# Decayed keys of a gated recurrence built by ACT in scaled blocks, and three GpSimd products moved to VectorE

## The chip, the cores and the metric

The kernel runs on one core of a Trainium2 chip. The metric is device time in microseconds (us) of one execution; the runs of the kernel before gave 2340.97, 2344.2 and 2345.61, with a median of 2344.2. The engines are named as in the profile: PE is TensorE's matmul, PEld its weight load, DVE VectorE, ACT ScalarE, POOL GpSimd, SP the engine that issues most DMAs.

## The reference

Two layers of a hybrid backbone work on 128 context tokens and 512 latent tokens of width 2048. Each layer normalises and modulates its input (adaLN), projects it to 6656 columns, and hands them to three groups of heads: windowed attention with rotary position (A), a gated linear recurrence in both directions (B), and a spatial gating MLP (C). Each branch is multiplied by its own gate and all are projected back. The change touches B and the rotary part of A. The recurrence, cut to what matters:

```python
def step(S, xs):                       # one chunk of 32 tokens
    qc, kc, vc, lfc = xs
    b = jnp.cumsum(lfc, axis=-2)
    qe = qc * jnp.exp(b)
    ke = kc * jnp.exp(-b)
    att = jnp.where(causal, jnp.einsum('bhtd,bhsd->bhts', qe, ke), 0.0)
    o = jnp.einsum('bhtd,bhdv->bhtv', qe, S) + jnp.einsum('bhts,bhsv->bhtv', att, vc)
    b_last = b[..., -1:, :]
    S = jnp.exp(b_last)[..., 0, :, None] * S + jnp.einsum('bhsd,bhsv->bhdv', kc * jnp.exp(b_last - b), vc)
    return S, o
```

and the rotary position of queries and keys of latent tokens:

```python
out = jnp.stack([x1 * cs - x2 * sn, x2 * cs + x1 * sn], axis=-2)
```

## The kernel before, in words

All 640 tokens (5 tiles of 128) stay on the chip. The input projection is split into blocks of columns. A block is either "rowmajor" (512 columns, tokens on the partitions of the result) or "colmajor" (128 columns, features on the partitions, tokens in halves of 384 and 256). Weights and inputs are each split in a high and a low part, and three matmuls make a product (L652 to L654, L660). The weight block `wr` comes by a DMA that SP issues, ACT rounds it to `wh` (L640), DVE subtracts to get `wl` (L641); four `wr` and three `wh` and `wl` buffers rotate.

All other work is laid beside this stream. A list `side` holds generators: the attention of a tile, the recurrence of a head, the gating MLP. The loops over weight blocks call `tick()`, which runs the first generator up to its next `yield`. A second list, the filler, makes the adaLN vectors of later use: DVE multiplies and adds blocks of `w_ada` as they land (L302, two of 512 columns for each block, 480 in all). The framework then orders each engine's instructions by priority (program order, with weight work raised) and by when it reckons the inputs ready; every engine runs its own list strictly in order. So a change of engine or of reckoned time moves instructions on all of them.

The recurrence handles a head at a time, four to a layer, with both directions d in one generator. `hgrn_prep` makes the cumulated gates, `qe` and the keys `e`, the chunk decays `Dt` (for each tile a 5x4 table a channel: how much chunk c's key has decayed for a query of chunk i), the end-of-tile decays `EG`, the keys `kd` for the state (L1044, DVE) and the queries `qB` for the state (L1045, POOL). Then the tile states are chained (L1067 transposes, L1068 copies on ACT, L1072 products, L1078 on DVE).

A loop over n makes the scores of tile n. A tile has four chunks of 32, and a query chunk i needs keys of chunks c <= i, decayed by `Dt[i, c]`. `build(j)` makes, for each direction, a buffer K of 128x512: four copies of the tile's 128 key columns, the i-th scaled chunk by chunk by row i of `Dt`; where c > i the factor is exp(-1e30), so 0, and where c = i it is 1. Before, this is one POOL product of 128x512 with broadcast operands (L1090). The score matmuls (L1105) take 32 query columns as weights and one of the four copies as moving data: four for each direction (two profile records each, as the operands are plain fp32). DVE keeps the causal part (L1108) and adds the directions (L1110); after one more yield PE transposes the sum (L1128), ACT copies it to `aT` (L1130), and three steps later the outputs are accumulated (L1117, L1120) and squared on ACT (L1123). There is one K buffer for each direction, so `build(n + 1)`, called right after the score matmuls of n, waits until they have read it. At the end the head's outputs are scaled on DVE (L1137), transposed on PE (L1143) and multiplied into the gate buffer B.

Three more products stand on POOL before: the two halves of rope (L751; DVE makes their terms in L748 and L749), the gate of each head in `b_gate` (L1004: B times the sigmoid), and `qB`. The sigmoid itself (`sigma`) is a minimum on DVE (L227), then a logarithm and an exponential on ACT (L228, L229). Elsewhere POOL multiplies the gates of the other branches (L1211), splits some activations (L622, L1229), scales the MLP (L1178, L1179) and adds the output (L1260).

## Time and profile before

| | |
|---|---|
| median of the runs | 2344.2 us |
| the profiled execution | 2338.18 us |
| its span, first to last instruction | 2336.4 us |
| PE busy | 2261.4 us (97%) |
| PEld busy | 1968.0 us (84%) |
| DVE busy | 1424.3 us (61%) |
| ACT busy | 778.7 us (33%) |
| POOL busy | 293.9 us (13%) |
| mean granted PE clock | 0.988 |

The span leaves out 1.8 us around the first and last instruction. PE's busy time is that of pipelined matmuls, whose records overlap: a stretch can show PE busy throughout and still run at different rates. A group's row gives its busy time in us, the mean of one in ns, then how long its engine had been idle before it and what ended that. In a row of the timeline the first number is the start, the second the duration from the first start to the last end of the merged instructions.

### The profile page before, as it was taken

How to read it: one execution, taken by the hardware profiler on the slowest of the kernel's cores; microseconds unless marked ns; L12 is line 12 of the kernel's file. 1: busy time of each engine (PE TensorE's matmuls, PEld its weight loads, DVE VectorE, ACT ScalarE, POOL GpSimd, SP SyncE). 2: the span in 40 equal slices, each digit the busy share in tenths (PEclk: the TensorE clock that was granted, in tenths of full speed). 3: DMA queues.
4: the chain of work that ended last, by engine and by line, in shares of the span. 5: the costliest groups of instructions: out<-in, count | busy, mean ns of one | idle time of the engine just before them, and what ended most of it. 6: DMA issues, size and time to landing. Idle time of an engine off the chain costs nothing.

```text
span 2336.4 us, 34944 instructions
## 1 busy us (share of the span) xinstructions
PE 2261.4 (97%) x13308; PEld 1968.0 (84%) x13308; DVE 1424.3 (61%) x2612; ACT 778.7 (33%) x1605; POOL 293.9 (13%) x234
## 2 busy tenths in 40 slices
PE   7999999999999989989999999999999999999999
PEld 5766678899999888977787878799999998998887
DVE  3436987768887766666667455855875942434223
ACT  3323434343334322332224234344343332223111
POOL 0000111002122211011112010101222220101110
PEclk9999999999999999999999999999999999999999
DMA  9675632434433354355552221322332323324332
GB/s 321 218 254 191 209 117 83 148 95 120 126 117 104 111 163 144 111 192 171 173 170 91 77 68 47 115 68 72 111 94 76 114 90 92 103 75 149 106 106 84
DMA packets 264876, 296.41 MB, mean 127 GB/s; under 512 B 17378, under 2 KB 166772, under 8 KB 262916
## 3 DMA queue, kind: packets, MB, share of 16 engines
q1 hardware_dynamic: 254368, 271.27, 37.2%
q10 hardware_dynamic: 10340, 22.91, 3.2%
q8 instruction: 104, 1.70, 0.3%
q14 instruction: 64, 0.52, 0.1%
HBM read 280.38 MB, written 13.73 MB: 126 GB/s over the span
## 4 chain that ended last, share of the span: by engine, by line
PE 75%; DVE 12%; DMA 7%; issue 2%; ACT 1%; POOL 0%; DVEq 0%; ACTq 0%; POOLq 0%
PE m L660 29%; PE m L652 11%; PE m L653 11%; PE m L654 11%; DMA wa<-in_w_ada_dram 6%; DVE aacc L302 4%; DVE wl L641 2%; PE s L240 2%; PE s L895 1%; PE s L941 1%; PE s L1105 1%; PE s L1072 1%; PE s L953 1%; PE s L954 1%; PE s L319 1%
## 5 line engine op out<-in xcount | busy, mean ns | idle before, releaser
L641 DVE TENSOR_TENSOR wl<-wr,wh 128x512 fp32r<-128x512 f32 (+1 forms) x535 | 401.5, 752 | 575.2 <-ACT wh L640 566.7
L640 ACT ACTIVATE wh<-wr 128x512 fp32r<-128x512 f32 (+1 forms) x535 | 336.1, 629 | 971.0 <-PE m L654 557.2
L652 PE MATMUL m<-wh,hh 128*128 128x512 f32 x1440 | 571.6, 397 | 9.2 <-DVE mg L1208 5.3
L653 PE MATMUL m<-wl,hh 128*128 128x512 f32 x1440 | 568.5, 395 | 3.5 <-DVE wl L641 3.5
L654 PE MATMUL m<-wh,hl 128*128 128x512 f32 x1440 | 565.6, 393 | 0.0
L660 PE MATMUL m<-hh,wh 128*128 128x384 f32 x2016 | 478.1, 317 | 0.0
L660 PE MATMUL m<-hl,wh 128*128 128x384 f32 x2016 | 465.0, 311 | 0.0
L660 PE MATMUL m<-hh,wl 128*128 128x384 f32 x2016 | 464.6, 311 | 0.0
L302 DVE SCALAR_TENSOR_TENSOR aacc<-wa,s,aacc 128x512 f32<-128x512 f32 x480 | 368.6, 801 | 72.9 <-DMA wa<-in_w_ada_dram 72.3
L652 PEld LDWEIGHTS m<-wh,hh 128*128 128x128 f32 x1440 | 272.0, 189 | 84.5 <-issue 10.3
L653 PEld LDWEIGHTS m<-wl,hh 128*128 128x128 f32 x1440 | 272.7, 189 | 64.2 <-DVE wl L641 7.4
L654 PEld LDWEIGHTS m<-wh,hl 128*128 128x128 f32 x1440 | 272.4, 189 | 59.0 <-issue 2.6
L660 PEld LDWEIGHTS m<-hh,wh 128*128 128x128 f32 x2016 | 312.5, 190 | 9.8 <-issue 8.1
L660 PEld LDWEIGHTS m<-hl,wh 128*128 128x128 f32 x2016 | 311.5, 189 | 0.4
L660 PEld LDWEIGHTS m<-hh,wl 128*128 128x128 f32 x2016 | 311.1, 189 | 0.3
L1090 POOL TENSOR_TENSOR mg<-ev,Dt 128x512 f32<-128x512 f32 x80 | 95.7, 1213 | 321.5 <-PE s L1105 107.2
L1260 POOL TENSOR_TENSOR mg<-mg,ev 128x512 f32<-128x512 f32 x30 | 43.9, 1473 | 287.9 <-DVE ev L1258 287.1
L751 POOL TENSOR_TENSOR mg<-g,g 128x256 f32<-128x256 f32 x32 | 32.8, 1047 | 263.8 <-DVE g L749 145.5
L925 ACT ACTIVATE g<-g,st,qs 128x384 f32<-128x384 f32 (+1 forms) x64 | 48.1, 752 | 36.0 <-DVE st L921 36.0
L228 ACT ACTIVATE ev<-ev 128x640 f32<-128x640 f32 x40 | 29.5, 738 | 72.3 <-DVE ev L227 71.2
L945 DVE TENSOR_TENSOR g<-s,g 128x512 fp32r<-128x512 f32 x56 | 38.4, 687 | 24.0 <-ACT g L944 18.1
L1045 POOL TENSOR_TENSOR g<-g,EG 128x512 f32<-128x512 f32 x16 | 22.7, 1416 | 239.4 <-DVE Dt L1030 125.1
(272 smaller groups left out, 1984.6 us busy)
## 6 DMA issues: line engine op xcount, KB each, us to landing
wr<-in_w_in_dram SPq DMA_DIRECT2D x406, 256.0 KB, 2.9
wa<-in_w_ada_dram SPq DMA_DIRECT2D x278, 256.0 KB, 3.0
wr<-in_w_out_dram SPq DMA_DIRECT2D x128, 256.0 KB, 2.9
wa<-in_w_ada_dram SPq DMA_DIRECT2D x16, 1024.0 KB, 6.7
wa<-in_w_in_dram SPq DMA_DIRECT2D x9, 1024.0 KB, 6.5
wa<-in_w_ada_dram SPq DMA_DIRECT2D x44, 128.0 KB, 3.3
mg<-const_xT_dram SPq DMA_DIRECT2D x4, 1280.0 KB, 5.8
x<-mg SPq DMA_DIRECT2D x20, 256.0 KB, 2.1
```

The source lines that it names most:

```text
L240: return self.nc.tensor.matmul(acc[32 * q:32 * q + 32, 0:n], lhsT=lhs[:, kk, :], rhs=rhs, start=kk < 4, stop=kk >= 12, skip_group_check=True)
L302: nc.vector.scalar_tensor_tensor(acc[:, cd], r, sc, acc[:, cd], op0=ALU.mult, op1=ALU.add)
L640: nc.scalar.activation(wh, raw, AF.Copy)
L641: nc.vector.tensor_tensor(wl, raw, wh.bitcast(F32), op=ALU.subtract)
L652: nc.tensor.matmul(ps, lhsT=hh, rhs=wh[:, 0], start=k == 0, stop=False)
L653: nc.tensor.matmul(ps, lhsT=hh, rhs=wl[:, 0], start=False, stop=False)
L654: nc.tensor.matmul(ps, lhsT=hl, rhs=wh[:, 0], start=False, stop=k == KT - 1)
L660: self.nc.tensor.matmul(ps[hf][:, 0:n], lhsT=w[:, a], rhs=h[:, o:o + n], start=k == 0 and i == 0, stop=k == KT - 1 and i == 2)
L925: nc.scalar.activation(dst[h], src[h], AF.Exp, bias=nmx[:, h:h + 1], scale=rq[:, h:h + 1], accum_out=den[:, h:h + 1])
L945: nc.vector.tensor_tensor(pt[1], pb, pt[0].bitcast(F32), op=ALU.subtract)
L1090: nc.gpsimd.tensor_tensor(k.rearrange("p (i c s) -> p i c s", i=4, c=4), bc(c4(pre[d][0])[:, j], 1, 4), bc(dd, 3, 32), op=ALU.mult)
L1260: (nc.vector if c == 3 else nc.gpsimd).tensor_tensor(xs, xs, y, op=ALU.add)
```

## The change

`build` no longer uses POOL. K's upper blocks (c > i) are zeroed once a layer by a DVE memset over both K buffers, since nothing writes there any more. For each key buffer ACT makes one copy of the four diagonal blocks (the key chunks unscaled, L1090 after) and six copies of 128x32 with a per-channel factor, one for each block below the diagonal (L1094). That is 14 ACT instructions a step in place of two POOL products; with 40 steps, 560 for 80. The rope halves, the gate and `qB` keep their form and move from POOL to DVE. Lines behind L1090 move down by three: L1105 is L1108 after, L1128 is L1131, L1143 is L1146.

```diff
@@ rope_ap
         for b, op in ((0, ALU.subtract), (1, ALU.add)):
-            nc.gpsimd.tensor_tensor(w(out)[:, :, :, b], w(t1)[:, :, :, b], w(t2)[:, :, :, b], op=op)
+            nc.vector.tensor_tensor(w(out)[:, :, :, b], w(t1)[:, :, :, b], w(t2)[:, :, :, b], op=op)
@@ b_gate
-        nc.gpsimd.tensor_tensor(self.B[:, h], self.B[:, h], s, op=ALU.mult)
+        nc.vector.tensor_tensor(self.B[:, h], self.B[:, h], s, op=ALU.mult)
@@ hgrn_prep
-        nc.gpsimd.tensor_tensor(c4(qB)[:, 1:5], c4(qe)[:, 1:5], bc(eg, 3, 32), op=ALU.mult)
+        nc.vector.tensor_tensor(c4(qB)[:, 1:5], c4(qe)[:, 1:5], bc(eg, 3, 32), op=ALU.mult)
@@ hgrn
             self.Cm = self.mg().rearrange("p (h t) -> p h t", h=4)
+            nc.vector.memset(self.Cm[:, 0:2, 0:512], 0.0)
@@ build
                 k = self.Cm[:, d, 0:512]
-                dd = pre[d][3][:, j, 0:4]
-                if d:
-                    dd = dd[:, :, ::-1]
-                nc.gpsimd.tensor_tensor(k.rearrange("p (i c s) -> p i c s", i=4, c=4),
-                                        bc(c4(pre[d][0])[:, j], 1, 4), bc(dd, 3, 32), op=ALU.mult)
+                blk = k.rearrange("p (a s) -> p a s", s=32)
+                e, dd = c4(pre[d][0])[:, j], pre[d][3][:, j]
+                nc.scalar.activation(blk[:, 3:13:3] if d else blk[:, 0:16:5], e[:, ::-1] if d else e, AF.Copy)
+                for i in range(1, 4):
+                    for c in range(i):
+                        q = 3 - c if d else c
+                        nc.scalar.activation(blk[:, 4 * i + q], e[:, q], AF.Copy, scale=dd[:, i, c:c + 1])
```

The order of the instructions, at the second score step of the second head in layer 0. First PE before: `mg` is K, `g` is `qe` of the one and the other direction, and `m` with `wh` and `wl` the weight stream.

```order
L660 MATMUL m_6033<-hh_1022,wl_6158 128x384
L660 MATMUL m_6034<-hh_1022,wl_6158 128x256
L1105 MATMUL s_6195<-mg_4873,g_5741 32x128 x4
L1105 MATMUL s_6201<-mg_4873,g_5949 32x128 x4
L660 MATMUL m_6033<-hh_1032,wh_6157 128x384
L660 MATMUL m_6034<-hh_1032,wh_6157 128x256
L660 MATMUL m_6033<-hl_1033,wh_6157 128x384
L660 MATMUL m_6034<-hl_1033,wh_6157 128x256
L660 MATMUL m_6033<-hh_1032,wl_6158 128x384
L660 MATMUL m_6034<-hh_1032,wl_6158 128x256
L319 MATMUL s_6217<-ones,aacc_5372 128x1 x8
```

And the same place on PE now:

```order
L660 MATMUL m_6094<-hh_1022,wl_6231 128x384
L660 MATMUL m_6095<-hh_1022,wl_6231 128x256
L1108 MATMUL s_6280<-mg_4873,g_5802 32x128 x4
L660 MATMUL m_6094<-hh_1032,wh_6230 128x384
L660 MATMUL m_6095<-hh_1032,wh_6230 128x256
L660 MATMUL m_6094<-hl_1033,wh_6230 128x384
L660 MATMUL m_6095<-hl_1033,wh_6230 128x256
L660 MATMUL m_6094<-hh_1032,wl_6231 128x384
L660 MATMUL m_6095<-hh_1032,wl_6231 128x256
L1108 MATMUL s_6286<-mg_4873,g_6010 32x128 x4
L319 MATMUL s_6314<-ones,aacc_5409 128x1 x8
```

The score matmuls of the two directions stood together; now six matmuls of the weight stream stand between them. Of the 40 steps, 28 are parted so, by 1 to 14 matmuls; before, none was.

ACT from the same step on, before (`aT` is the transposed score, `junk` the square of an output):

```order
L640 ACTIVATE wh_6296<-wr_6294 128x512
L640 ACTIVATE wh_6355<-wr_6353 128x512
L987 ACTIVATE ev_6228<-m_6033 128x384
L987 ACTIVATE ev_6228<-m_6034 128x256
L1130 ACTIVATE aT_6253<-s_6251 128x128
L228 ACTIVATE ev_6228<-ev_6228 128x640
L229 ACTIVATE ev_6228<-ev_6228 128x640
L640 ACTIVATE wh_6414<-wr_6412 128x512
L1130 ACTIVATE aT_6308<-s_6306 128x128
```

and now, from the third step's first key on:

```order
L640 ACTIVATE wh_6476<-wr_6474 128x512
L987 ACTIVATE ev_6325<-m_6094 128x384
L987 ACTIVATE ev_6325<-m_6095 128x256
L1090 ACTIVATE mg_4873<-ev_5025 128x4x32
L1094 ACTIVATE mg_4873<-ev_5025,Dt_5812 128x32 x6
L1090 ACTIVATE mg_4873<-ev_5211 128x4x32
L1094 ACTIVATE mg_4873<-ev_5211,Dt_6020 128x32 x6
L228 ACTIVATE ev_6325<-ev_6325 128x640
L640 ACTIVATE wh_6535<-wr_6533 128x512
L229 ACTIVATE ev_6325<-ev_6325 128x640
L1133 ACTIVATE aT_6350<-s_6348 128x128
L1090 ACTIVATE mg_4873<-ev_5025 128x4x32
```

The 14 key instructions of a step now stand in ACT's list between the weight casts, the evacuation of the next head's gate (L987) and its sigmoid (L228, L229), so a key of the next step waits behind whatever these wait for.

## The prediction

> **What bounds the kernel now.** I read the head of the page first, then the waits of PE, then the busy time by stretches, then the groups that the change touches, and last the timeline of one recurrence step.
>
> ```profile
> span 2336.4 us, 34944 instructions
> PE 2261.4 (97%) x13308; PEld 1968.0 (84%) x13308; DVE 1424.3 (61%) x2612; ACT 778.7 (33%) x1605; POOL 293.9 (13%) x234
> ```
>
> PE is busy for 97% of the span, so an edit that adds no matmul can gain only from PE's idle time (75 us in all) and from the slow clock that follows a stall. The next view is who PE waited for (total us, times, longest).
>
> ```profile
> PE s L1143 <- DVE g L1137: 10.4, 6, 6.1
> ...
> PE s L941 <- DVE g L930: 8.7, 6, 3.2
> PE s L1072 <- ACT g L1068: 7.7, 2, 4.1
> ...
> PE s L1128 <- DVE att L1108: 1.9, 1, 1.9
> ...
> PE s L833 <- POOL g L751: 0.3, 1, 0.3
> ```
>
> Two things stand here. PE hardly ever waits for POOL: 0.3 us. POOL's key building (L1090), which the change takes away, ends no wait of PE at all. And where PE waits in the recurrence and the attention, the engine named is mostly DVE. So the moved work is not on the path; it can matter only by what POOL does to DVE, and by what ACT and DVE do with the work that they take over.
>
> ```profile
> 404.00:408.00 4.00, 0.89 (x7) 0.62 (x5) 2.11 (x8) 2.86 (x11) 0.30 (x1) 1.00 0.24 91
> 408.00:410.00 2.00, 1.92 (x8) 1.84 (x9) 0.61 (x4) 0.39 (x1) 0.00 (x0) 0.52 0.38 112
> 410.00:412.00 2.00, 2.00 (x6) 0.93 (x4) 0.69 (x1) 0.73 (x2) 0.00 (x0) 0.62 0.16 59
> ```
>
> These are stretches around one 3.2 us stall (PE, PEld, DVE, ACT, POOL busy, then the granted clock). After it the clock is 0.52 and 0.62 for two stretches of 2 us: 0.96 + 0.76 = 1.7 us more are lost. A stall of a few us therefore costs about half as much again.
>
> **What leaves POOL.**
>
> ```profile
> L1090 POOL TENSOR_TENSOR mg<-ev,Dt 128x512 f32<-128x512 f32 x80 | 95.7, 1213 | 321.5 <-PE s L1105 107.2 <-DVE ev L1039 94.7 <-issue 83.9
> ...
> L751 POOL TENSOR_TENSOR mg<-g,g 128x256 f32<-128x256 f32 x32 | 32.8, 1047 | 263.8 <-DVE g L749 145.5 <-PE s L955 92.8 <-issue 25.5
> ...
> L1045 POOL TENSOR_TENSOR g<-g,EG 128x512 f32<-128x512 f32 x16 | 22.7, 1416 | 239.4 <-DVE Dt L1030 125.1 <-issue 114.3
> ...
> L1004 POOL TENSOR_TENSOR mg<-mg,ev 128x640 f32<-128x640 f32 x8 | 13.7, 1711 | 60.4 <-ACT ev L229 38.9 <-DVE g L1037 13.6 <-DVE aacc L302 7.9
> ...
> L751 POOL TENSOR_TENSOR g<-g 128x128 f32<-128x128 f32 x16 | 9.3, 592 | 303.3 <-DVE g L749 257.8 <-issue 40.6 <-PE m L654 4.3
> ```
>
> 95.7 + 32.8 + 22.7 + 13.7 + 9.3 = 174 us of POOL's 294, or 59%.
>
> **What that gives back to DVE.** For the DVE lines that run beside POOL, the mean of a group stands above its median or its minimum; I read the excess as time held up by POOL.
>
> ```profile
> L641 DVE TENSOR_TENSOR wl<-wr,wh 128x512 fp32r<-128x512 f32 (+1 forms) x535 | 401.5, 752 | 575.2 <-ACT wh L640 566.7
> ...
> L302 DVE SCALAR_TENSOR_TENSOR aacc<-wa,s,aacc 128x512 f32<-128x512 f32 x480 | 368.6, 801 | 72.9 <-DMA wa<-in_w_ada_dram 72.3
> ```
> ```profile
> L1110 DVE TENSOR_TENSOR asum<-att,att 128x128 f32<-128x128 f32 x40 | 24.1, 603 | 0.8
> ...
> L1044 DVE TENSOR_TENSOR g<-ev,Dt 128x640 f32<-128x640 f32 x16 | 18.3, 1142 | 0.8 <-ACT Dt L1032 0.7
> ...
> L748 DVE TENSOR_TENSOR g<-mg,rope 128x256 f32<-128x256 f32 x32 | 17.6, 550 | 0.0
> ...
> L748 DVE TENSOR_TENSOR g<-ev,rope 128x128 f32<-128x128 f32 x16 | 4.9, 307 | 0.1
> ```
>
> The same lines with minimum/median/maximum (ns):
>
> ```profile
> L641 DVE TENSOR_TENSOR wl<-wr,wh x535: 415/692/2057, 34.0 to 2322.2; 128x512 fp32r<-128x512 f32 x178, 128x256 fp32r<-128x256 f32 x1
> ```
> ```profile
> L302 DVE SCALAR_TENSOR_TENSOR aacc<-wa,s,aacc x480: 715/745/2064, 207.3 to 1861.5; 128x512 f32<-128x512 f32 x160
> ```
> ```profile
> L1110 DVE TENSOR_TENSOR asum<-att,att x40: 264/739/1137, 571.5 to 1886.6; 128x128 f32<-128x128 f32 x40
> ```
> ```profile
> L1044 DVE TENSOR_TENSOR g<-ev,Dt x16: 811/826/1675, 533.1 to 1857.8; 128x640 f32<-128x640 f32 x16
> ```
> ```profile
> L748 DVE TENSOR_TENSOR g<-mg,rope x32: 408/417/960, 288.8 to 1479.4; 128x256 f32<-128x256 f32 x32
> ```
>
> 535 x (752 - 692) = 32; 480 x (801 - 745) = 27; 40 x (603 - 264) = 14; 16 x (1142 - 826) = 5; 32 x (550 - 417) = 4, and as much for L749, its twin: 86 us. Shared out by POOL's busy time, the moved operations own 59% of it: 51 us. The new DVE work is 32 rope halves at 0.417 = 13 us, 16 of the keys' rope at 0.307 = 5, 16 products of 512 columns at 0.826 x 512/640 = 0.66, so 11, 8 gates of 640 columns at 0.826 = 7, and two memsets that I bound by 1 us each: 38 us. DVE comes out about 13 us lighter, all of it in the recurrence; in the rope stretches it is even, since four operations at 0.55 become six at 0.417 (2.2 against 2.5 us a tile).
>
> The Trainium skill, "SBUF — State Buffer", section "Who interferes with whom", says that a VectorE operation with two SBUF inputs and a GpSimd operation that reads SBUF exclude each other wholly, the second waiting until the first has finished. The trace agrees only in part: L1110 goes from 264 to a median of 739 ns, a hold-up of 0.48 us, which is less than half of a POOL operation of 1.2 us. By the rule the relief could be as much as the 174 us of POOL time; by the rows it is 51.
>
> **What of it reaches PE.** The 1.9 us at L1128 is a late DVE (L1108) just beside key builds: I take -1.9 (0 to -1.9). Of the 10.4 us at L1143, 6.1 are one wait, and there DVE was in adaLN adds (L302), which wait for their own DMA (72.3 us); of the other 4.3 I take -3 (0 to -10.4 for the whole). The 7.7 us at L1072 come through ACT's L1068, queued behind a gate that waits for DVE, again behind L302: 0 (0 to -7.7). The 8.7 at L941 follow the rope bursts, which do not get shorter: 0 (-8.7 to +3, the latter if the burst, 0.3 us a tile longer in 8 of its tiles, lands on PE). Sum -4.9, with half as much again for the clock: **-7.3 us**.
>
> **What the split keys cost PE.** By the new order, PE runs the four score matmuls of direction 0, then other matmuls, then those of direction 1, in 28 of the 40 steps; before they stood together in all 40. The load rows show what a change of kind costs:
>
> ```profile
> 650.05 0.30 PEld L660 LDWEIGHTS m<-hh,wl 128*128 128x128 f32 x2
> 650.55 0.39 PEld L1105 LDWEIGHTS s<-mg,g 128*32 128x32 f32 x16 [0.20 <-issue]
> 651.14 0.30 PEld L660 LDWEIGHTS m<-hh,wh 128*128 128x128 f32 x2 [0.20 <-issue]
> ```
>
> Entering and leaving the group idles the loads 0.20 us each. A split adds one entry and one exit; as matmuls overlap loads, I take one of the two: 28 x 0.20 = **+5.6 us** (0, if the array hides both, to 28 x 0.40 = 11).
>
> **What ACT takes.** 80 copies of four blocks and 480 scaled blocks of 128x32, a shape that the trace of before doesn't have.
>
> ```profile
> L640 ACT ACTIVATE wh<-wr 128x512 fp32r<-128x512 f32 x533 | 335.3, 630 | 971.0 <-PE m L654 557.2 <-PE m L660 326.2 <-issue 30.5
> ...
> L382 ACT ACTIVATE hh<-mg,gs 128x512 fp32r<-128x512 f32 x16 | 11.3, 708 | 0.0
> ...
> L382 ACT ACTIVATE hh<-mg,gs 128x128 fp32r<-128x128 f32 x16 | 6.3, 391 | 9.0 <-DVE gs L288 9.0
> ...
> L1033 ACT ACTIVATE EG<-G 128x25 f32<-128x25 f32 x16 | 3.5, 220 | 4.5 <-DVE G L1027 4.5
> ```
>
> L382 scales by a column, as the new blocks do. Its two forms give (708 - 391)/384 = 0.83 ns a column, so 32 columns take 391 - 96 x 0.83 = 0.31 us; L1033, without a scale column, bounds it from below at 0.22, L382 from above at 0.39. Four unscaled blocks: 391 less 78 (708 - 630, the price of the column) = 0.31 too. Neighbours overlap:
>
> ```profile
> 662.28 0.28 ACT L1123 ACTIVATE junk<-s 128x128 bf16<-128x128 f32 x1 [2.48 <-PE s L1117]
> 662.46 0.19 ACT L1123 ACTIVATION_READ_ACCUMULATOR junk<-s 128x1 f32 x1
> ```
>
> The second starts 0.18 after a first of 0.28, so 0.10 is hidden, and a block occupies ACT 0.21 us. The Trainium skill, "ScalarE: Activation LUTs", section "What ACT_TABLE_LOAD costs", gives 186 ns + 0.833 ns a column, 93 more for a pointer operand and 93 of overlap; by that estimate it is 0.21 as well, and the sum would not change. No run here shows the new shape yet.
>
> A step has two keys: 14 x 0.21 = 2.9 us. Beside them ACT does a weight cast (0.63 - 0.10), aT (0.18) and the square with its accumulator (0.27): 3.9 us. PE's step:
>
> ```profile
> 648.02 0.38 PEld L1105 LDWEIGHTS s<-mg,g 128*32 128x32 f32 x16 [0.20 <-issue]
> ```
> ```profile
> 656.77 0.65 PE L1105 MATMUL s<-mg,g 128*32 128x128 f32 x16
> ```
> ```profile
> 661.18 0.64 PE L1105 MATMUL s<-mg,g 128*32 128x128 f32 x16
> ```
>
> 4.41 us from group to group, but only 650.55 - 648.02 = 2.5 from the first to the second. In the long steps ACT fits with 0.5 us over; in the short one direction 1's key is about 0.3 + 2.9 = 3.2 us after the first group and so late by 0.7, which the new order covers by 3 to 9 other matmuls (0.15 each, from 0.30 a pair). I take **0** for PE's waits on keys, because the row nearest to the new form is L382 and its step fits; the cover is 0.5 us a step, and the upper end is rival 2's. ACT grows by 560 x 0.21 = 118 us, a third on its 779.
>
> **The sum.** -7.3 + 5.6 + 0 = -1.7 us on the profiled execution (2338.18, of which 2336.4 are the span). The median of the runs is 2344.2, 6.0 above that execution; the difference is carried over: 2344.2 - 1.7 = 2342.5, so **2342 us**. About 0.2%, 4.7 us, is what a measurement of this kernel can tell from no change. The ends of the terms give (1.9 + 4.3 + half of 8.7) x 1.5 = -15.8 with free splits at best, and +11 with no relief at worst; as both ends seldom come whole, the forecast's own range is 2331 to 2353.
>
> **Rival 1, faster: the port frees DVE's whole queue.** If POOL holds DVE up more than my excess shows, the backlog behind which L1137, L1068 and L1108 stand goes too. The condition is that the adaLN adds come earlier, and with them their buffers and their next DMAs. Price: (10.4 + 7.7 + 1.9) x 1.5 = 30, less 5.6 for the splits: -24, so 2320 us. For it: L302 has a maximum of 2064 ns against a median of 745. Against it: 72.3 us of waits that are DMA's. By the skill's exclusive lock, named above, this would be the case; the trace bears it out in half, so 0.2.
>
> **Rival 2, slower: ACT's queue makes the keys late.** ACT runs in order, and gates of the next head stand between the builds.
>
> ```profile
> ACT ev L228 <- DVE ev L227: 71.2, 35, 5.5
> ```
>
> A gate waits 2.0 us for DVE on average, and now keys are queued behind it, for which PE waits; POOL had no such neighbour. It decides where ACT's step passes 4.41 us: with blocks at 0.25 instead of 0.21 the 0.5 us are gone, and without any overlap 14 x 0.31 + 0.63 + 0.28 + 0.47 = 5.7 us make 1.3 us x 24 long steps + about 1 x 8 short ones = 39 us. Half of that, or a 2 us gate in 10 of the 40 steps, is +20: 2364 us. Chance 0.2.
>
> **Rival 3: nothing comes back.** DVE's lateness is the DMA's alone and stays where it is; the splits cost 5.6: 2350 us, on the edge between no change and slower. Chance 0.1.
>
> **How the numbers follow.** Forecast 0.5, rivals 0.2, 0.2, 0.1. The forecast's range lies by 0.2 below 2339.5, by 0.25 within and by 0.05 above 2348.9; rival 3 gives half to each side of that edge. Faster: 0.2 + 0.2 = 0.40; same: 0.25 + 0.05 = 0.30; slower: 0.05 + 0.2 + 0.05 = 0.30. The range reaches to the middles of rivals 1 and 2, with a tenth beyond either: 2320 to 2364.
>
> **What would show it.** Right: L1110 near 264 ns throughout, L641 and L302 near their medians; L1094 at about 0.31 us and 0.21 apart; PE's wait at L1131 (now L1128) gone, no wait of PE on an ACT key above 1 us; L1108 in groups of eight. Wrong: PE waiting for L1094 in most steps, with the clock falling after it (rival 2), or the waits at L1146 and L1075 (now L1143 and L1072) gone as well (rival 1). A stall of a new kind in the attention would be outside all four.

## The result, and the profile after

The changed kernel takes 2316.97 us (median of 4 runs, 2315.74 to 2319.98) where the kernel before took 2342.59 (4 runs, 2340.47 to 2345.61): a ratio of 0.9892, with a 95% interval of 0.9874 to 0.9909. That is 25.6 us faster, where 2342 had been forecast with a range down to 2320. The profiled execution took 2315.77 us. The head of its page:

```profile
span 2313.9 us, 35246 instructions
...
PE 2255.9 (97%) x13308; PEld 1958.9 (85%) x13308; DVE 1391.7 (60%) x2686; ACT 894.0 (39%) x2165; POOL 120.6 (5%) x82
```

DVE took over 74 instructions and is busy for 32.6 us less. ACT grew by 115 us (118 was forecast), and PE's time is not longer for it. The waits of PE (total us, times, longest):

```profile
PE m L652 <- DVE mg L1211: 6.2, 1, 6.2
PE s L1146 <- DVE g L1140: 6.0, 2, 5.4
PE s L1196 <- DVE mg L1197: 5.4, 1, 5.4
PE s L1073 <- ACT g L1069: 4.1, 2, 2.2
...
PE s L941 <- DVE g L930: 1.3, 4, 0.4
```

L1146 is L1143 of before: 10.4 us have become 6.0. L1073 was L1072: 7.7 have become 4.1. The 8.7 us at L941 have become 1.3. The first and third rows stood at 5.3 and 5.1 us before (behind L1208 and L1194 there). The rows of the operations that the change touches, and of those beside them:

```profile
L302 DVE SCALAR_TENSOR_TENSOR aacc<-wa,s,aacc 128x512 f32<-128x512 f32 x480 | 354.6, 770 | 76.9 <-DMA wa<-in_w_ada_dram 76.2 <-DVE wl L641 0.5
...
L1094 ACT ACTIVATE mg<-ev,Dt 128x32 f32<-128x32 f32 x480 | 113.0, 309 | 9.4 <-PE s L1108 9.2
...
L748 DVE TENSOR_TENSOR g<-mg,rope 128x256 f32<-128x256 f32 x32 | 13.4, 418 | 0.0
L751 DVE TENSOR_TENSOR mg<-g,g 128x256 f32<-128x256 f32 x32 | 12.2, 419 | 0.1
...
L1113 DVE TENSOR_TENSOR asum<-att,att 128x128 f32<-128x128 f32 x40 | 11.5, 288 | 0.6
```

ACT's new blocks alone, with minimum, median and maximum (ns), and who waited for them (us, times):

```profile
L1094 ACT ACTIVATE mg<-ev,Dt x480: 302/307/323, 529.1 to 1863.1; 128x32 f32<-128x32 f32 x160
...
  PEld s L1108: 5.3, 27
```

L748 runs at 418 ns in the mean (550 before), the sum of the scores (L1113, L1110 before) at 288 (603 before), and the new blocks at 309 ns, the forecast 0.31 us. DMA's own share of L302's waits is what it was (76.2 us against 72.3).

**Where the time went.** Set beside each other at the same weight matmul, the two executions run level up to 280 us. The changed one is 10 us ahead by 530 us (first attention), 17 ahead by 1340 (recurrence), 20 by 1400 (second attention), 22.4 by 1895, and then keeps its lead. Two things make that up. The gaps in which neither PE nor PEld runs, added up from the instruction records, fell from 60.4 to 43.6 us: 16.8. And PE was at half clock in 16 windows of 3.41 us before, in 11 now: 5 windows, each worth half its length, 8.5 us. Together 25.3; the span lost 22.5, which leaves 2.8 us by which PE's work itself got longer.

### The profile page after: what moved, and what is told of

Read it like the earlier page. It is cut to its first block, busy times and chain, and to the rows that moved or that the text cites. A ratio compares the mean times of both kernels' runs of the same rounds, so it can differ in the third digit from the quotient of the medians.

```text
span 2313.9 us, 35246 instructions
## 1 busy us (share of the span) xinstructions
PE 2255.9 (97%) x13308; PEld 1958.9 (85%) x13308; DVE 1391.7 (60%) x2686; ACT 894.0 (39%) x2165; POOL 120.6 (5%) x82
## 4 chain that ended last, share of the span: by engine, by line
PE 53%; DVE 6%; DMA 3%; issue 1%; ACT 1%; DVEq 0%; ACTq 0%
PE m L660 21%; PE m L653 9%; PE m L652 9%; PE m L654 9%; DMA wa<-in_w_ada_dram 3%; DVE aacc L302 2%; DVE wl L641 1%; PE s L895 1%; PE s L941 1%; PE s L1108 1%; DVE ev L1261 0%; PE s L319 0%; PE s L1196 0%; PE s L953 0%; PE s L954 0%
## 5 line engine op out<-in xcount | busy, mean ns | idle before, releaser
L641 DVE TENSOR_TENSOR wl<-wr,wh 128x512 fp32r<-128x512 f32 (+1 forms) x535 | 386.9, 725 | 569.2 <-ACT wh L640 562.3
L302 DVE SCALAR_TENSOR_TENSOR aacc<-wa,s,aacc 128x512 f32<-128x512 f32 x480 | 354.6, 770 | 76.9 <-DMA wa<-in_w_ada_dram 76.2
L660 PEld LDWEIGHTS m<-hh,wh 128*128 128x128 f32 x2016 | 311.1, 189 | 13.6 <-issue 12.1
L1094 ACT ACTIVATE mg<-ev,Dt 128x32 f32<-128x32 f32 x480 | 113.0, 309 | 9.4 <-PE s L1108 9.2
L1214 POOL TENSOR_TENSOR mg<-mg,ev 128x640 f32<-128x640 f32 x16 | 26.6, 1663 | 1513.8 <-ACT ev L229 1493.2
L944 ACT ACTIVATE g<-s 128x512 fp32r<-128x512 f32 x56 | 32.5, 596 | 57.5 <-PE s L941 54.1
L945 DVE TENSOR_TENSOR g<-s,g 128x512 fp32r<-128x512 f32 x56 | 38.4, 688 | 23.4 <-ACT g L944 17.0
L1111 DVE COPY_PREDICATED att<-m,s 128x128 f32<-128x128 uint8 x80 | 22.8, 301 | 39.8 <-PE s L1108 39.0
```

The lines of the kernel that those rows point to most:

```text
L302: nc.vector.scalar_tensor_tensor(acc[:, cd], r, sc, acc[:, cd], op0=ALU.mult, op1=ALU.add)
L641: nc.vector.tensor_tensor(wl, raw, wh.bitcast(F32), op=ALU.subtract)
L660: self.nc.tensor.matmul(ps[hf][:, 0:n], lhsT=w[:, a], rhs=h[:, o:o + n], start=k == 0 and i == 0, stop=k == KT - 1 and i == 2)
L944: nc.scalar.activation(pt[0], pb, AF.Copy)
L945: nc.vector.tensor_tensor(pt[1], pb, pt[0].bitcast(F32), op=ALU.subtract)
L1094: nc.scalar.activation(blk[:, 4 * i + q], e[:, q], AF.Copy, scale=dd[:, i, c:c + 1])
```

## The experiments

Theory 1: POOL's two-input products hold up DVE's, and DVE's late results stop PE; taking the products off POOL gives that time back, whoever does them. Theory 2: the gain comes from the new order of instructions and shorter chains, and the hold-up is off the path. Each ratio is to the kernel before on the same chip.

| run | what | median us | before us | ratio, 95% interval |
|---|---|---|---|---|
| p_rope | before, rope to DVE | 2321.45 | 2341.93 | 0.9912 (0.9900 to 0.9925) |
| p_gates | before, gates and queries to DVE | 2337.0 | 2341.93 | 0.9975 (0.9963 to 0.9986) |
| p_keys | before, keys to ACT | 2340.53 | 2341.93 | 0.9988 (0.9979 to 0.9997) |
| hog | after, scratch products of the operands on POOL | 2342.33 | 2341.93 | 0.9996 (0.9987 to 1.0005) |
| hog_results | after, scratch products of the results on POOL | 2332.89 | 2338.73 | 0.9970 (0.9960 to 0.9980) |
| hog_writes | after, memsets on POOL, too many | 2373.02 | 2338.73 | 1.0135 (1.0117 to 1.0153) |
| hog_writes2 | after, memsets on POOL | 2312.82 | 2341.7 | 0.9881 (0.9864 to 0.9897) |
| hog_rope | after, scratch products beside rope alone | 2338.94 | 2341.7 | 0.9985 (0.9971 to 1.0000) |
| rope_w1 | before, rope's products on POOL made short writes | 2329.05 | 2340.66 | 0.9954 (0.9940 to 0.9967) |
| rope_w3 | the same, long writes | 2328.64 | 2340.66 | 0.9947 (0.9935 to 0.9959) |
| k3 | after, one more key buffer | 2309.14 | 2338.73 | 0.9868 (0.9850 to 0.9887) |
| keys_dve | after, keys on DVE | 2309.54 | 2341.7 | 0.9865 (0.9850 to 0.9881) |
| allv_keysdve | keys_dve, POOL empty | 2290.96 | 2341.7 | 0.9786 (0.9770 to 0.9802) |
| allv_k3 | k3, POOL empty | 2287.47 | 2338.73 | 0.9778 (0.9760 to 0.9795) |

### One part of the change alone

p_rope:

```diff
-            nc.gpsimd.tensor_tensor(w(out)[:, :, :, b], w(t1)[:, :, :, b], w(t2)[:, :, :, b], op=op)
+            nc.vector.tensor_tensor(w(out)[:, :, :, b], w(t1)[:, :, :, b], w(t2)[:, :, :, b], op=op)
```

> The kernel before, with one part of the change alone: the 32 half products of rope (L751) go from GpSimd to VectorE; gates, queries and keys stay on GpSimd. The two traces show that the time was gained in two kinds of stretch: about 13 us in the two attentions (280-530 us and the like in layer 1), about 9 us net in the recurrences. Theory 1 (hold-up: GpSimd's two-input products hold up VectorE's and are themselves held up, the worst of them 3746 ns, and the late result reaches TensorE through ScalarE): rope alone brings the attention's 13 us, so 2327 to 2333 us against 2342.6. Theory 2 (the prediction's term: the rope bursts only change hands, VectorE's own work takes the place of what it waited): 2340 to 2345 us. The order on TensorE changes a little here too (808 of 12,405 instructions stand elsewhere), so a gain does not yet tell hold-up from order; another run of this set does.

p_gates:

```diff
-        nc.gpsimd.tensor_tensor(self.B[:, h], self.B[:, h], s, op=ALU.mult)
+        nc.vector.tensor_tensor(self.B[:, h], self.B[:, h], s, op=ALU.mult)
...
-        nc.gpsimd.tensor_tensor(c4(qB)[:, 1:5], c4(qe)[:, 1:5], bc(eg, 3, 32), op=ALU.mult)
+        nc.vector.tensor_tensor(c4(qB)[:, 1:5], c4(qe)[:, 1:5], bc(eg, 3, 32), op=ALU.mult)
```

> The kernel before, with one part of the change alone: the gate products (L1004) and the decayed queries (L1045) go to VectorE. The order on TensorE is that of before, instruction for instruction, so any difference is of when things get ready. Theory 1 (hold-up): these 24 instructions carried some 22 of the 108 us by which VectorE's instructions beside GpSimd ran over their own free median, and the waits of TensorE on VectorE in the recurrence (L1146 behind L1140 10.4 us, L1072 behind L1069 7.7) shrink in part: 2 to 5 us are gained, 2337.5 to 2340.5 us. Theory 2 (hold-up off the path): within 1.5 us of 2342.6.

p_keys is the change's memset and its `build`, and nothing else:

```diff
-                nc.gpsimd.tensor_tensor(k.rearrange("p (i c s) -> p i c s", i=4, c=4),
-                                        bc(c4(pre[d][0])[:, j], 1, 4), bc(dd, 3, 32), op=ALU.mult)
+                nc.scalar.activation(blk[:, 3:13:3] if d else blk[:, 0:16:5], e[:, ::-1] if d else e, AF.Copy)
...
+                        nc.scalar.activation(blk[:, 4 * i + q], e[:, q], AF.Copy, scale=dd[:, i, c:c + 1])
```

> The kernel before, with one part of the change alone: the decayed keys as scaled block copies on ScalarE; rope, gates and queries stay on GpSimd. The key products of TensorE come apart in the same way as in the full change (28 of 40 steps in two groups of four). Theory 1 (hold-up): the 40 products of L1090 were the largest holder of VectorE in the recurrence (28 of 108 us); with them gone L1110 is back near 290 ns and the recurrence gains 6 to 10 us less 5.6 us for the groups that come apart: 2336 to 2343 us. Theory 2 (the recurrence loses only the 5.6 us of the split groups, nothing comes back): 2347 to 2349 us. A queue on ScalarE that makes keys late would show as TensorE waiting for L1094 in many steps and 2355 us or more.

Measured: rope alone gains 0.88%, 20.5 us, more than even theory 1 gave it. The gates and queries gain 0.25%, the keys 0.12%. The three add up to 1.25%, where the whole change gives 1.08%. Rope, 42 us of the 174 us that left POOL, brings four fifths of the gain; the keys, 96 us of it, gain next to nothing once the split groups are paid for (5.9 us, below). p_gates has PE's order of before, instruction for instruction, so its 0.25% owes nothing to PE's order. The remaining long waits of PE in p_rope are those of the recurrence:

```profile
PE s L1143 <- DVE g L1137: 11.3, 7, 6.8
PE s L166 <- DVE g L159: 9.7, 1, 9.7
PE s L1072 <- ACT g L1068: 7.0, 2, 3.7
```

L941 and L252 are gone from its first waits: in neither attention is there a gap of PE above 0.4 us, where before has 1.7 us at 296, 0.7 at 329, 3.2 at 405, 1.5 at 452 and 3.2 at 1383.

### Putting POOL's reads back, in the order of after

hog leaves the changed kernel as it is and makes POOL read the same operands into a tile that nobody uses:

```diff
             nc.vector.tensor_tensor(w(out)[:, :, :, b], w(t1)[:, :, :, b], w(t2)[:, :, :, b], op=op)
+            for i in range(nh // 2):
+                nc.gpsimd.tensor_tensor(self.hog.rearrange("p (h a e) -> p h a e", h=2, a=2),
+                                        w(t1)[:, 2 * i:2 * i + 2, :, b], w(t2)[:, 2 * i:2 * i + 2, :, b], op=op)
...
+                for i in range(4):
+                    nc.gpsimd.tensor_tensor(self.hog.rearrange("p (c s) -> p c s", c=4), e, bc(dd[:, i, 0:4], 2, 32), op=ALU.mult)
```

> The full change, and beside each product that it moved GpSimd reads the same operands again and writes products of them into a scratch tile that nobody uses (4 products of 128x128 for each key block, 5 for each gate, 4 for each decayed query, 1 or 2 for each half of rope). Order on TensorE and VectorE is that of the full change, instruction for instruction; GpSimd's reads are put back, its results are no longer waited for. Theory 1, in full (hold-up of VectorE by GpSimd's reads is what was gained): VectorE's instructions beside the scratch products run at 0.5 to 1.2 us again and most of the time comes back: 2330 to 2342 us against 2317.0 of the full change. Theory 1b (what was gained is the late results of GpSimd itself, the chain through them): VectorE runs long again but the time stays near 2317 to 2322. Theory 2 (the new order on TensorE brought the gain): 2315 to 2319, as the full change.

Measured: 2342.33 us, all of the gain gone. Its lines stand a little further down: L749 and L750 are the rope terms, L752 the halves, L754 the scratch products.

```profile
L754 POOL TENSOR_TENSOR hog<-g,g 128x128 f32<-128x128 f32 x64 | 35.8, 560 | 267.1 <-DVE g L750 263.5
...
L752 DVE TENSOR_TENSOR mg<-g,g 128x256 f32<-128x256 f32 x32 | 19.6, 646 | 0.1
...
L750 DVE TENSOR_TENSOR g<-mg,rope 128x256 f32<-128x256 f32 x32 | 17.2, 538 | 0.0
L749 DVE TENSOR_TENSOR g<-mg,rope 128x256 f32<-128x256 f32 x32 | 15.6, 487 | 0.0
```

The rope halves that take 419 ns on DVE in the changed kernel take 646 here, with PE's and DVE's lists unchanged. The waits of PE show where it lands:

```profile
PE s L945 <- DVE g L934: 12.1, 7, 4.3
...
PE m L661 <- DVE g L1386: 3.1, 1, 3.1
```

L945 is L941 of before, whose 8.7 us are back as 12.1; the 3.1 us stand at 411, in the first attention. So theory 2 alone falls: the new order without the relief is worth nothing. hog reads for longer than the moved products did (POOL 402 us, before 294), but DVE suffers less by it than before: summed over all DVE instructions that overlap a POOL one, the excess over the free median of their shape is 81 us, against 108 before and 41 after.

hog_results separates two ways in which that can act: POOL slows DVE, or POOL keeps the operand buffers. Its edit, against hog:

```diff
             for i in range(nh // 2):
-                nc.gpsimd.tensor_tensor(self.hog.rearrange("p (h a e) -> p h a e", h=2, a=2),
-                                        w(t1)[:, 2 * i:2 * i + 2, :, b], w(t2)[:, 2 * i:2 * i + 2, :, b], op=op)
+                o = w(out)[:, 2 * i:2 * i + 2, :, b]
+                nc.gpsimd.tensor_tensor(self.hog.rearrange("p (h a e) -> p h a e", h=2, a=2), o, o, op=op)
```

> The full change with scratch products on GpSimd again, as many as in the run before, but each reads the finished result (rope's output half, the gated B, the decayed query) instead of the operands, so that no operand buffer is held until GpSimd has read it; the key's scratch products still read the decay factors, which live for the whole head anyway. Order on TensorE and VectorE as in the full change. The scratch products that read operands gave 2342.3 us, all of the gain gone; two causes fit: VectorE's instructions take longer beside GpSimd's reads (theory 1), or VectorE waits for operand buffers that GpSimd has not yet read (theory 1c). Theory 1: 2336 to 2345 us. Theory 1c: 2315 to 2324 us.

Measured: 0.9970, between the two expectations. Of the distance from 0.9892 to hog's 0.9996, three quarters are lost without rope's operands being held. Held buffers, or POOL's somewhat smaller load here (379 us), explain at most the last quarter. Held buffers are the less likely of the two: in hog's trace no instruction is seen waiting for a scratch product. What does differ is that the reads come later here, so that the rope halves take 452 ns, where hog has 646.

hog_writes replaces the reads by writes. Its helper, called in the places of hog_results' products:

```diff
+    def wfill(self, o):
+        self.nc.gpsimd.tensor_tensor(self.hog[:, 0:1], o, o, op=ALU.mult)
+        for _ in range(2):
+            self.nc.gpsimd.memset(self.hog, 0.0)
```

> The same places as the run that reads results, but each scratch product of 128x128 becomes one product of a single column, which waits for the result, and two memsets of 128x128 on GpSimd, which write and read nothing. Order on TensorE and VectorE as in the full change. If it is GpSimd's reading that holds VectorE up (theory 1, the shared read port): 2315 to 2321 us, VectorE's two-input products at their free medians beside the memsets. If any GpSimd work that touches SBUF does it: 2330 us or more. If the gain were due to GpSimd's sequencing alone (semaphores, waits), also 2330 or more.

The run missed its purpose: 2373 us, slower than any other. The cause is its own making, as the waits of PE and the idle time of an evacuation on DVE show:

```profile
PE s L1125 <- DVE att L1128: 18.6, 3, 8.0
PE m L666 <- DVE ev L997: 13.4, 2, 8.0
```
```profile
L104 POOL MEMSET hog<- 128x128 f32 x1008 | 212.0, 210 | 58.8
...
L997 DVE COPY ev<-m 128x384 f32<-128x384 f32 x8 | 4.4, 555 | 41.9 <-POOL hog L102 41.9
```

With four waiting products and eight memsets for each key, POOL needs 4 x 0.25 + 8 x 0.21 = 2.7 us a key, 5.4 for a step of 4.4, falls behind, and DVE waits for a buffer that POOL has still to read. hog_writes2 mends that (against hog_writes; the 6 is the number of memsets behind one waiting product):

```diff
-                for i in range(4):
-                    self.wfill(e[:, 0, 0:1])
+                self.wfill(e[:, 0, 0:1], 6)
```

> The run with memsets, mended: there each key block had four waiting products and eight memsets on GpSimd, some 2.9 us for one block, so that GpSimd itself ran late in the recurrence and TensorE waited 18.5 us at the key products. Now one waiting product of a single column and as many memsets of 128x128 as keep GpSimd's time per place below that of the scratch products (6 for a key block, 8 for a gate, 10 for a query, 2 or 1 for a half of rope). Order on TensorE and VectorE as in the full change. Theory 1 (reads of GpSimd hold up VectorE, writes alone do not): 2315 to 2322 us where the full change stands at 2317, VectorE's products at their free medians. If GpSimd's activity as such costs: 2330 us or more.

Measured: 2312.82 us, 0.9881, the time of the changed kernel, with 784 memsets and 165 us of writing on POOL (here L754, L755 are the rope terms and L757 the halves):

```profile
L104 POOL MEMSET hog<- 128x128 f32 x784 | 164.6, 210 | 45.3
...
L755 DVE TENSOR_TENSOR g<-mg,rope 128x256 f32<-128x256 f32 x32 | 13.5, 421 | 0.0
L754 DVE TENSOR_TENSOR g<-mg,rope 128x256 f32<-128x256 f32 x32 | 13.5, 421 | 0.0
L757 DVE TENSOR_TENSOR mg<-g,g 128x256 f32<-128x256 f32 x32 | 12.3, 421 | 0.1
```

So POOL's reading costs, and its writing does not. This is what the Trainium skill, "SBUF — State Buffer", section "Who interferes with whom", states: a VectorE instruction with two SBUF inputs contends with a GpSimd instruction that reads SBUF, not with one that only writes it. The runs agree. The same page of the Trainium skill, section "Summary: rules for kernel authors", adds that the second to issue fully blocks until the first has finished. For DVE behind a POOL product the traces bear this out too, as the last section shows.

hog_rope puts the reads back beside rope alone; the edit is the first hunk of hog without the others.

> The full change, with scratch products on GpSimd beside rope alone (80 products of 128x128 that read the halves' operands and write a tile that nobody uses); gates, queries and keys are left as in the full change. Order on TensorE and VectorE is that of the full change. Rope's part of the change alone had gained 20.5 us, but it also moved 808 instructions on TensorE. Theory 1 (hold-up in the rope bursts): 10 to 20 us of the gain are lost, 2327 to 2337 us where the full change stands at 2317, with stalls at L945 in both attentions and the halved clock behind them. Theory 2 (rope's gain is the new order): within 3 us of the full change.

Measured: 2338.94 us, 0.9985. With a sixth of hog's scratch time (45 of 282 us) it takes back 22 of the 25 us, a little more than the 10 to 20 of theory 1, by stalls of 3.8 us at 312, 3.1 at 412, 4.3 at 1383 and 2.9 at 1488. The reads beside rope are what cost.

### The hold-up in the order of before

hog shows the hold-up in the order of after. These two keep the order of before, but for 7 and 67 instructions on PE (rope_w1 as shown, rope_w3 with `range(3)`). Both leave the rotation out, so rope's outputs are zero:

```diff
-            nc.gpsimd.tensor_tensor(w(out)[:, :, :, b], w(t1)[:, :, :, b], w(t2)[:, :, :, b], op=op)
+            nc.gpsimd.tensor_tensor(w(out)[:, 0:1, 0, b, 0:1], w(t1)[:, 0:1, 0, b, 0:1], w(t2)[:, 0:1, 0, b, 0:1], op=op)
+            for _ in range(1):
+                nc.gpsimd.memset(w(out)[:, :, :, b], 0.0)
```

> The kernel before, with each of rope's 48 half products on GpSimd (1.05 us, two operands read) replaced by a product of a single column, which waits for the same operands, and one memset of the same output (the rotation is left out, its outputs are zero). Order on TensorE, VectorE, ScalarE and SyncE is that of before but for 7 instructions on TensorE and one on VectorE. Theory 1 (hold-up, in whatever order): VectorE's L748 and L749 all near 0.42 us, 12 to 20 us faster than before, 2320 to 2329 us. Theory 2 (rope's gain needs the new order): within 4 us of before.

> As the run before, with three memsets of the same output in place of one, so that GpSimd's result comes about as late as the product's did (some 0.25 + 3 x 0.28 us against 1.05), still without reading more than a column (the rotation is left out again; 67 instructions on TensorE stand elsewhere). If VectorE's hold-up is the cost (theory 1a): as rope_w1, within 4 us. If it is GpSimd's own result that came too late (theory 1b): most of it is lost again, within 6 us of before.

Measured: 0.9954 and 0.9947, 10.8 and 12.4 us; rope_w1 stays just short of the 12 of theory 1. In rope_w1 the two gaps of 3.2 us at 405 and 1383 are gone, and L941 (L943 here) is down from 8.7 us:

```profile
PE s L943 <- DVE g L932: 2.7, 6, 1.1
```

The cause is the burst of rope products on DVE before that wait: from the first to the last product of L748 and L749 it takes 9.3 us at 393 in the kernel before and 6.2 here, with the same instructions in it. The gap at 296 stays (1.9 us). In rope_w3 POOL needs 0.39 + 3 x 0.31 = 1.3 us for a result, 0.5 more than in rope_w1, and the time is the same: it is not POOL's usual duration, but the hold-up that goes with its reads, that cost the 11 to 12 us. The other 8 to 10 of rope's 20.5 us came only in p_rope, where POOL is out of the chain altogether and PE's order differs. One place where POOL stood in the chain shows in the timeline of before:

```profile
290.40 3.75 POOL L751 TENSOR_TENSOR mg<-g,g 128x256 f32<-128x256 f32 x1 [25.46 <-issue]
```
```profile
296.64 1.20 DVE L641 TENSOR_TENSOR wl<-wr,wh 128x512 fp32r<-128x512 f32 x1
297.33 0.60 ACT L908 ACTIVATE g<-s 128x512 f32<-128x512 f32 x1 [2.48 <-POOL mg L751]
...
297.82 0.27 ACT L245 ACTIVATE g<-s 128x128 f32<-128x128 f32 x1
...
298.14 0.38 PE L252 MATMUL s<-misc,g 128*128 128x2 f32 x2 [1.71 <-ACT g L245]
```

POOL's first product took 3.75 us while DVE ran its own two-input products back to back (the median is 0.92): the hold-up works both ways. ACT's L908 waited 2.5 us for POOL, ACT's L245 stood behind it, and PE waited 1.7 us for that. The view of waits names only the last link, ACT. In rope_w1 this link is still there (ACT waits 2.7 us for POOL, PE 1.9 for ACT). How much of these 8 to 10 us is POOL's place in the chain and how much the 808 instructions that rope's move shifts on PE, no run tells: none has the order of p_rope with POOL still in the chain and no reads. That the order has a part is seen at the old gap of 405: the L941 behind it comes after 1220 matmuls of the weight stream in before and in rope_w1, after 1265 in p_rope and in the changed kernel.

### What the split keys cost, and what ACT was needed for

k3 gives direction 0 a second key buffer in idle columns of `Cm`:

```diff
+            nc.vector.memset(self.Cm[:, :, 512:640], 0.0)
...
+                alt = d == 0 and j % 2
+                row = (lambda i: self.Cm[:, i, 512:640]) if alt else (lambda i, d=d: self.Cm[:, d, i * P:(i + 1) * P])
```

> The full change, with a second buffer for the keys of direction 0 in columns of Cm that stand idle during the recurrence (the other direction still has one buffer). TensorE's key products then stand in one group of eight in 33 of 40 steps instead of 12. Theory (the split of a group costs 0.20 us, 28 of them in the full change): 21 splits less, 4.2 us gained, 2313 us (2311 to 2315.5) against 2317.0. Rival: the splits are hidden by stalls that are there anyway: 2316 to 2318.

keys_dve makes the keys as one product on DVE:

```diff
-                nc.scalar.activation(blk[:, 3:13:3] if d else blk[:, 0:16:5], e[:, ::-1] if d else e, AF.Copy)
...
+                nc.vector.tensor_tensor(k.rearrange("p (i c s) -> p i c s", i=4, c=4),
+                                        bc(c4(pre[d][0])[:, j], 1, 4), bc(dd, 3, 32), op=ALU.mult)
```

> The full change but for the keys: one product of 128x512 for each step and direction on VectorE (40 of them) in place of the 560 copies on ScalarE; GpSimd is left with the other 80 products. VectorE gets 40 times 0.69 us (27.6 us) in the recurrences, ScalarE loses 115 us, and TensorE's key products come apart in 1 step instead of 28 (5.4 us by 0.20 us each). If VectorE has the room once nothing holds it up (theory 1): 2308 to 2316 us. Rival: VectorE, 70 to 80% busy in the recurrence, gets late and TensorE waits for it at L1108 or L1146: 2322 us or more.

Measured: 0.9868 and 0.9865, which is 5.6 and 6.3 us better than the change's 0.9892. 21 and 27 splits less would give 4.4 and 5.7 us; the intervals overlap the change's a little, so this supports the price and does not fix it. The price stands in the timeline of after, around a split step:

```profile
637.91 0.43 PE L1108 MATMUL s<-mg,g 128*32 128x128 f32 x8
...
639.34 0.43 PE L1108 MATMUL s<-mg,g 128*32 128x128 f32 x8
```

Twice 0.43 us, where an undivided group of before took 0.65 and 0.64: a split costs 0.21 us. In keys_dve the product, which the expectation counted 40 times, stands 80 times, and DVE had the room for all of them:

```profile
L1090 DVE TENSOR_TENSOR mg<-ev,Dt 128x512 f32<-128x512 f32 x80 | 55.5, 694 | 0.0
```

So ACT was not needed for the keys: either engine would do.

### POOL empty

allv_k3 is k3 with the remaining products of POOL on DVE as well, allv_keysdve is keys_dve with the same edit:

```diff
-            (nc.vector if t % 2 else nc.gpsimd).tensor_tensor(v, v, gb, op=ALU.mult)
+            nc.vector.tensor_tensor(v, v, gb, op=ALU.mult)
...
-            (eng or nc.gpsimd).tensor_tensor(dst, dst, s.rearrange("p (t q) -> p t q", q=P), op=ALU.mult)
+            (eng or nc.vector).tensor_tensor(dst, dst, s.rearrange("p (t q) -> p t q", q=P), op=ALU.mult)
```

> The run with the second key buffer, and the remaining arithmetic of GpSimd also on VectorE (L622, L1181, L1182, L1214, L1232, L1263: 80 products, 118 us on GpSimd, beside which VectorE's instructions ran 41 us over their free medians). If hold-up works wherever GpSimd reads (theory 1): TensorE's waits for L1211 (6.2 us) and L1197 (5.4 us), with the slow clock behind each, shrink by a half or more; 2300 to 2310 us. Rival: VectorE gets 60 to 70 us of work of its own where it is already late, in the gates at the end of a layer: 2313 to 2325 us.

> As the run before, and the remaining arithmetic of GpSimd on VectorE too, so that GpSimd does no arithmetic at all. The same step, with the keys on ScalarE and the second key buffer, ended at 0.978 of the kernel before. Theory 1 (additive): 0.976 to 0.981 of before, 2285 to 2297 us. Rival (VectorE out of room): 0.985 or more, 2307 us or more.

Measured: 2287.47 us, 0.9778, faster than either theory had it, and 2290.96, 0.9786. They are not told apart; both beat the kernel before and the changed one. The page of allv_k3:

```profile
span 2284.0 us, 35174 instructions
...
PE 2241.9 (98%) x13308; PEld 1956.8 (86%) x13308; DVE 1399.2 (61%) x2762; ACT 899.1 (39%) x2213; POOL 0.7 (0%) x8
```

DVE has 76 instructions more than after and is busy for only 7.5 us longer, as the 41 us of hold-up that were left are gone too. PE's gaps fall from 43.6 to 27.8 us, and PE's wait for L1211 from 6.2 to 2.5:

```profile
PE m L652 <- DVE mg L1217: 2.5, 1, 2.5
```

## Why the prediction was wrong

**The failed step** is in "What of it reaches PE": "The 8.7 at L941 follow the rope bursts, which do not get shorter: 0". The 8.7 us became 1.3, and rope alone, put at nothing, brought 20.5. The premise held: the burst at 393 took 9.3 us before and takes 9.5 in the changed kernel, with eight halves and one weight split (L641) more in it. The conclusion did not follow from it. First, the wait was as long as the hold-up: without POOL's reads and without the halves the burst takes 6.2 us (rope_w1), 3.1 less, and the 3.2 us of PE's wait at 405 are gone, in the order of before. Second, in the changed kernel DVE spends that time on the halves, and there PE reaches the L941 of that wait 45 weight matmuls later; the step had left PE's order in the attention out. This order is not enough by itself: hog and hog_rope have it too, and with POOL's reads back PE waits 12.1 and 12.4 us at that line.

**"So the moved work is not on the path"** was drawn from PE's 0.3 us of waits for POOL, and was wrong too; what followed it, that the work "can matter only by what POOL does to DVE", is the larger part of the answer. A row of waits names the last link. The link before it, ACT's L908 behind POOL's L751, is in the timeline, and hog, by POOL's reads alone, puts the whole loss back without touching PE's list.

**The relief of DVE.** The forecast was 51 us of hold-up removed for 38 us of new work. DVE's busy time fell by 32.6 us, not 13. The excess fell by 108 - 41 = 67 us. The text had found 86 us of it on five kinds of lines and given 59% to the moved products, by POOL's time; they had 67 of 108. So the share was about right, and the sum too small. The new work came out near its forecast (34 us in the rows of L751, L1045 and L1004, without the memsets).

**The length of a hold-up.** "The trace agrees only in part" misread its row. L1110 starts 0.44 us into a POOL product of 1.05 us and ends 0.14 us after it (lines in the last section); it was held to that product's end, and its 0.48 us are less than the product because part of it was over. The chance of 0.2 for rival 1 rested on this reading.

**The range.** The terms give ends of -1.9, -10.4, -7.7 and -8.7 us. Taken whole, with the half for the clock, they make 43 us and reach 2301. The sum of the best end took 4.3 of the 10.4, half of the 8.7 and none of the 7.7, and the forecast's range began at 2331.

**L1143, L1072, L1128.** -3 was taken for L1143; it lost 4.4. 0 was taken for L1072, "again behind L302", whose waits were put down to its own DMA; it lost 3.6, though L302's waits for its DMA did not change. L1128's 1.9 (L1131 after) went as forecast. These misses are small beside rope's.

**The clock.** A half was added to every stall. Five half-speed windows less made 8.5 us beside 16.8 us of gaps: right in the sum, though the single stalls don't behave so (below).

**The split keys** were +5.6 us; the rows give 0.21 us a split, 5.9 for 28 (k3 and keys_dve agree with it).

**ACT's keys** were at 0.31 us and kept no matmul waiting: the weight loads (PEld) waited for them 27 times, 5.3 us in all, and PE's own list has none. Rival 2 falls. Rival 3 falls by p_gates alone. Rival 1 came nearest: its 2320 us are 3 from the result. Its mechanism, POOL's hold-up, is right; its place was not, since L1143 and L1072 lost 8 of 18 us and the attention, for which no rival had a term, gave most. That its time is so near is luck.

## What to carry to other kernels

What a product that leaves POOL is worth does not show in PE's waits for POOL (0.3 us here): look at DVE's two-input instructions beside it, and at where their burst stands before a PE wait, not at who ends that wait. Rank such moves by place: 42 us of POOL time in rope were worth 20 us, 96 us in the keys some 8, before the price of the splits. A cheap test of contention is a scratch load in the unchanged order, once reading and once only writing.

## What the hardware showed that was not expected

**The clock drops by windows.** In the records PE's clock is either full or half, and half only in stretches of 3.41 us or multiples, all on one grid through the execution. The windows of that grid around four stalls of before (PE, PEld, DVE, ACT, POOL busy, then the granted clock):

```profile
295.45:298.87 3.42, 1.71 (x11) 1.21 (x10) 3.42 (x5) 0.77 (x2) 3.42 (x4) 1.00 0.27 79
298.87:302.28 3.41, 3.41 (x12) 2.93 (x12) 3.41 (x6) 0.09 (x1) 2.65 (x3) 0.50 0.26 74
...
404.68:408.09 3.41, 0.22 (x3) 0.01 (x1) 1.56 (x6) 2.61 (x11) 0.00 (x0) 1.00 0.30 112
408.09:411.51 3.42, 3.42 (x12) 2.75 (x12) 1.21 (x4) 1.12 (x2) 0.00 (x0) 0.50 0.23 71
...
452.47:455.88 3.41, 1.91 (x16) 1.94 (x16) 3.34 (x9) 0.73 (x3) 0.00 (x0) 1.00 0.67 218
455.88:459.29 3.41, 3.41 (x25) 3.04 (x23) 2.88 (x6) 2.37 (x5) 0.00 (x0) 1.00 0.49 146
...
1380.89:1384.31 3.42, 1.89 (x9) 1.23 (x7) 2.20 (x6) 1.68 (x7) 1.43 (x2) 1.00 0.16 59
1384.31:1387.72 3.41, 1.76 (x9) 1.31 (x10) 1.42 (x7) 1.60 (x6) 0.00 (x0) 1.00 0.29 77
1387.72:1391.13 3.41, 3.41 (x17) 2.50 (x17) 1.39 (x2) 1.50 (x3) 0.00 (x0) 1.00 0.28 77
```

Of these, the windows with PE busy for 0.22 and 1.71 us are followed by one at half clock, which costs 1.7 us; those with 1.76, 1.89 and 1.91 are not. So a stall of 1.7 us at 296 cost as much again, and one of 3.2 us at 1383 cost nothing beyond itself, because it lay across two windows. The Trainium skill, "TensorE: Matmul & The Clock Gate", section "What's actually happening", gives a free-running window of 3413 ns and a clock of half or full; the trace agrees, and in these windows about half a window of idling decides. Over all the runs the edge is not sharp: windows with PE busy for 0.43 to 0.58 of their length went either way (in rope_w1 none follows the stall at 296, with 0.44), and in hog, hog_writes and p_keys four windows at half clock follow one with PE busy throughout. What set those off is open; PE's ends are modelled.

**The hold-up lasts to the end of POOL's product.** Two pairs, the first from before (the first of a step's two key products and the sum of the scores), the second from hog (a scratch product and a rope half):

```profile
648.63 1.05 POOL L1090 TENSOR_TENSOR mg<-ev,Dt 128x512 f32<-128x512 f32 x1 [9.54 <-PE s L1105]
```
```profile
649.07 0.75 DVE L1110 TENSOR_TENSOR asum<-att,att 128x128 f32<-128x128 f32 x1
```
```profile
298.11 0.52 POOL L754 TENSOR_TENSOR hog<-g,g 128x128 f32<-128x128 f32 x1
```
```profile
298.24 0.68 DVE L752 TENSOR_TENSOR mg<-g,g 128x256 f32<-128x256 f32 x1
```

POOL's products end at 649.68 and 298.63, DVE's at 649.82 and 298.92: 0.14 and 0.29 us later by these rounded rows. In before, 161 instructions of L641, L302, L748, L749, L1110 and L1044 start while a POOL product runs. 147 of them end behind it, by a time that goes with their own width alone: in the median 0.15 us for 128 columns, 0.28 for 256, 0.55 for 512 and 0.68 for 640, wherever in POOL's product they had started. The other 14 fall into POOL products of 2.1 us and more, like the one of 3.75 us above: there DVE's instructions ran at their free time and POOL's lasted until they were through. So a long duration on POOL can itself be a wait for DVE, and it is no measure of what DVE loses beside it.
